# A second chain of adding transfers in the room of spent input combinations, a product ahead of two attention tiles, and a fixed order for the joining

## The chip, the cores and the metric

The kernel runs on one core of one Trainium2 chip, in one launch. The metric is the device time in microseconds, as the median of several runs. A profile is one such execution taken by the hardware profiler; its span, from the first to the last record, is a little shorter than its time.

## The reference

One decoder layer for a sequence of 256 tokens of width 1024 (all float32):

```python
mod = silu(c) @ w_ada + b_ada                # shift, scale, gate: 1024 each
h = rmsnorm(x, norm_g) * (1 + scale) + shift
q, k, v, g_attn, cb, cc, cx, g_conv, m_attn, m_conv = split(h @ w_in)   # ten blocks of 1024 columns
attn = softmax(q k^T / sqrt(128) + bias, causal) v         # 8 heads of 128, one block of 256 keys
y_attn = (attn * silu(g_attn)) @ w_o_attn
y_conv = (cb * conv3(cc * cx) * silu(g_conv)) @ w_o_conv
merged = sigmoid(m_attn) * y_attn + sigmoid(m_conv) * y_conv
return rmsnorm(x + gate * (merged @ w_out), final_g)
```

## The kernel before

**Precision.** Each product of float32 matrices is three products in fp32r: a matrix is split into a high part (ScalarE, "ACT", copies it to fp32r: the `h` tiles of line 74) and a low part (VectorE, "DVE", subtracts: the `l` tiles of line 75), and TensorE ("PE") takes high times high, high times low, low times high. So every MB of weights costs one ACT copy and one DVE subtraction of 128x2048 elements ahead of its matmuls. The `h` and `l` tiles stand in rings of three buffers each: the split of one unit can begin when the matmuls of the unit three before it are done. The raw weights come through a ring of five buffers of 1 MB (`RAW_BUFS`), loaded from SP's queue; a buffer is free when its split is done.

**The work in order.** Adaptive norm; q and k; v; then twelve units of 256 columns for `cc`, `cx`, `cb` with the attention heads between them; four units `gc`, four `ga`; from here on the stage that the change touches. It holds `m_conv` (named `mc`), `m_attn` (tiles `ma00` to `ma11`), `w_o_attn` (tiles `oa00` to `oa11`), `w_o_conv` (`oc`) and `w_out` (`o00` to `o11`). A tile such as `ma01` is 512 of the 1024 rows of the weight against 512 columns, for both halves of the tokens: 24 matmuls. Two tiles make one half of the columns.

**Seven products.** `mc` and `oc` are computed with seven products of 12 matmuls each where eight would be usual (a Strassen-Winograd scheme, class `Seven`, methods `p7 p5 p1 p6 p2 p4 p3`; on PE the products show as `mcp7h`, `ocp3l` and so on). Four of the seven take combinations of the input's quarters (`combos`: two big tiles, `sxhV` and `sxhBI` for `mc`, `sxcV` and `sxcBI` for `oc`; the first of the two holds what p7 and p5 read, the second what p6 and p3 read). Some take sums of weight blocks, and these sums are made by transfers that add: POOL's queue loads one block into the tile `sum` (shown as `mcsum`, `ocsum`, line 544) and adds another to it (line 509); the tile `first` (`mct`, `oct`) is loaded on SP and added to by POOL. `p7` reads `sum`, then POOL adds a third block for `p6`, and DVE adds one more for `p4`. Both chains use the same big tile, named by its tag W2, so `ocsum` waits until `mcp4l` (the low part of `mc`'s p4) has read `mcsum`.

**Joining.** `SA` becomes sigmoid(m_attn) times y_attn, `SC` becomes sigmoid(m_conv) times y_conv (lines 634 and 620). `joined(n)` (line 687) adds them for one half n of the columns, `turned(n)` transposes the sum on PE (`pm`, line 711) and splits it into `M` (lines 353 and 354), and `M` times w_out gives `ao`. `wo_split` loads and splits w_out; for its second half the last 256 columns are multiplied with the gate first (line 700, `gf`). The gate is a column tile `gcol`; to get it as a row, PE transposes it (`pgt`), ACT copies it (`grow`), ACT's queue stores it (`gd`) and loads it back to all partitions (`gf`, line 683), which takes W2 after `ocsum`.

**What sets the order.** The tile framework sorts each engine's instructions by priority and readiness, except those wrapped in `pin`, which keep the order of the program. PSUM banks come from a ring of five (`bank`), apart from banks 0 to 2, which the seven products hold.

Of the kernel before, what the change touches and what calls it, by code (L numbers as in the profile page):

```python
# [11 lines left out]
F32 = mybir.dt.float32  # L12
F32R = mybir.dt.float32r
AF = mybir.ActivationFunctionType
ALU = mybir.AluOpType
PSUM = bass.MemoryType.PSUM

P = 128
D = 1024
S = 256  # L20
NH = 8
KT = D // P
# [13 lines left out]
UNIT = {key: i for i, key in enumerate(UNITS)}  # L36
# [3 lines left out]
def layer_kernel(ctx: ExitStack, tc, x, c, vec, wp_all, slab_all, onehot, final_g, out):  # L40
    nc = tc.nc
    x, out = x[0], out[0]

    const = ctx.enter_context(tc.tile_pool(name="const", bufs=1))
    big = ctx.enter_context(tc.tile_pool(name="big", bufs=1))
    wp = ctx.enter_context(tc.tile_pool(name="wp", bufs=3))
    tp = ctx.enter_context(tc.tile_pool(name="tp", bufs=2))
# [6 lines left out]
    def bank(name, at=None):  # L54
        if at is None:
            at = ring[turn[0] % len(ring)]
            turn[0] += 1
        return ps.tile([P, 512], F32, tag=f"b{at}", name=name)
# [19 lines left out]
    pin = tc.keep_in_program_order  # L78

    H = big.tile([P, KT, 512], F32R, tag="H", name="H")  # L80
    QK = big.tile([P, 2 * NH, S], F32, tag="QK", name="QK")
    V = big.tile([P, 2, D], F32, tag="V", name="V")
# [7 lines left out]
    ident = const.tile([P, P], F32, name="ident")  # L90
# [6 lines left out]
    gcol = const.tile([P, KT], F32, name="gcol")  # L97
# [181 lines left out]
    for i in range(KT):  # L279
# [7 lines left out]
        a, b = span(0), span(1)  # L287
# [64 lines left out]
    def put(src, dst, j, pin=lambda i: i):  # L352
        pin(nc.scalar.activation(dst[:, 2 * j:2 * j + 2, 0:S], src, AF.Copy))  # L353
        pin(nc.vector.tensor_sub(dst[:, 2 * j:2 * j + 2, S:], src, dst[:, 2 * j:2 * j + 2, 0:S].bitcast(F32)))
# [111 lines left out]
    n = 0  # L466
# [25 lines left out]
    def gated(blk, src, dst, j):  # L492
        g = unit((blk, j), H, tmp("cc", f"{blk}{j}"))
        sg = tmp("y", f"s{blk}{j}")
        nc.scalar.activation(sg, g, AF.Silu)
        nc.vector.tensor_mul(sg, sg, src[:, 2 * j:2 * j + 2, :])
        put(sg, dst, j)
# [8 lines left out]
        return [bank(f"a{blk}{n}{t}") for t in range(2)]  # L506

    def add_on(t, key):
        nc.gpsimd.dma_start(t, wp_all[UNIT[key]], accum_op=ALU.add)

    def combos(x, name):
        f = raw_tile([P, 2048], "f" + name).rearrange("p (k n) -> p k n", k=KT)
        nc.vector.tensor_add(f, x[:, :, 0:S].bitcast(F32), x[:, :, S:].bitcast(F32))
        out = {}

        def quarter(t, kh):
            return f[:, 4 * kh:4 * kh + 4, t * P:(t + 1) * P]

        def combo(i, op, a, b, tag):
            v = tp.tile([P, 4, P], F32, tag=tag, name=f"v{name}{i}", bufs=2)  # L520
            op(v, a, b)
            dst = homes[i // 3][:, i % 2]
            nc.scalar.activation(dst[:, :, 0:P], v, AF.Copy)
            nc.vector.tensor_sub(dst[:, :, P:], v, dst[:, :, 0:P].bitcast(F32))
            out[i] = dst
            return v

        homes = [big.tile([P, 2, 4, S], F32R, tag=tag, name=f"sx{name}{tag}") for tag in ("V", "BI")]
        v1 = combo(1, nc.vector.tensor_sub, quarter(1, 0), quarter(1, 1), "cx")
        combo(0, nc.vector.tensor_sub, quarter(0, 0), quarter(1, 0), "cc")  # L530
        v2 = combo(3, nc.vector.tensor_sub, v1, quarter(0, 0), "y")
        combo(4, nc.vector.tensor_add, v2, quarter(0, 1), "cx")
        return {3: out[0], 1: out[1], 2: out[3], 4: out[4]}

    class Seven:
        def __init__(self, blk, x, sink):
            self.blk, self.x, self.sink = blk, x, sink

        def key(self, r, c):
            return (self.blk, c - 1, r - 1)  # L540

        def begin(self):
            self.sum = big.tile([P, 2048], F32, tag="W2", name=self.blk + "sum")
            nc.gpsimd.dma_start(self.sum, wp_all[UNIT[self.key(1, 2)]])  # L544
            add_on(self.sum, self.key(2, 2))

        def begin_first(self):
# [65 lines left out]
    def part(x, t, n):  # L613
        return x[:, t, 512 * n:512 * (n + 1)]
# [9 lines left out]
    def tile(blk, n, kh):  # L624
        if kh == 0:
            banks[blk] = pair(blk, n)
        a = banks[blk]
        rows_tile(blk, n, kh, GA if blk == "oa" else H, a)
        if kh and blk == "ma":
            for t in range(2):  # L630
                nc.scalar.activation(part(SA, t, n), a[t], AF.Sigmoid)
        elif kh:
            for t in range(2):
                nc.vector.tensor_mul(part(SA, t, n), part(SA, t, n), a[t])

    mc, oc = Seven("mc", H, to_gate), Seven("oc", GC, to_merge)
    mc.begin()
    ring[:] = range(3, 8)
    turn[0] = 0
    for j in range(4):  # L640
        gated("gc", YB, GC, j)
        if j < 2:
            run_slot(n + j)
        if j == 1:
            mc.begin_first()
            mc.sx = combos(H, "h")
    SC = big.tile([P, 2, D], F32, tag="YB", name="SC")
    gated("ga", AT, GA, 0)
    mc.p7()
    gated("ga", AT, GA, 1)  # L650
    mc.p5()
    gated("ga", AT, GA, 2)
    mc.p1()
    mc.p6()
# [2 lines left out]
    mc.p2()  # L657
    tile("ma", 0, 0)
    mc.p4()
    oc.begin()  # L660
    tile("ma", 0, 1)
    mc.p3()
    oc.sx = combos(GC, "c")
    tile("ma", 1, 0)
    oc.begin_first()
    oc.p7()
    tile("ma", 1, 1)
    oc.p5()
# [3 lines left out]
    tile("oa", 0, 1)  # L672
    oc.p2()
    oc.p4()
    gf = big.tile([P, 2 * D], F32, tag="W2", name="gf")
    gb, fg = gf[:, 0:D], gf[:, D:]
    pgt = bank("pgt")
    nc.tensor.transpose(pgt[0:KT, 0:P], gcol, ident)
    grow = tp.tile([KT, P], F32, tag="mx", name="grow")
    nc.scalar.activation(grow, pgt[0:KT, 0:P], AF.Copy)  # L680
    gd = tc.dram_tile([KT, P], F32, name="gd")
    nc.scalar.dma_start(gd, grow)
    nc.scalar.dma_start(gb, bass.AP(tensor=gd.tensor, offset=gd.offset, ap=[[0, P], [1, D]]))

    def joined(n, ts=range(2)):
        for t in ts:
            nc.vector.tensor_add(part(SA, t, n), part(SA, t, n), part(SC, t, n))

    joined(0)
    tile("oa", 1, 0)  # L690
    oc.p3()
    M = big.tile([P, KT, 512], F32R, tag="H", name="M")
    wo = {}
# [1 line left out]
    def wo_split(n, kh, pin=lambda i: i):  # L695
        raw = load(("wo", n, kh), f"wo{n}{kh}").rearrange("p (k n) -> p k n", k=4)
        if n:
            g = gb[:, D - S:]
            g = bass.AP(tensor=g.tensor, offset=g.offset, ap=[g.ap[0], [0, 4], g.ap[1]])
            pin(nc.vector.tensor_mul(raw[:, :, S:], raw[:, :, S:], g))  # L700
        wo[n, kh] = split(raw, [P, 4, 512], f"o{n}{kh}", 1, pin)
# [3 lines left out]
    def turned(n):  # L705
        for j in range(2 * n, 2 * n + 2):
            pm = bank(f"pm{j}")
            for k in range(2 * j, 2 * j + 2):
                for t in range(2):
                    c0 = (k % 2) * S + t * P  # L710
                    nc.tensor.transpose(pm[:, c0:c0 + P], MR[:, t, k * P:(k + 1) * P], ident)  # L711
            put(pm.rearrange("p (a b) -> p a b", a=2), M, j)

    turned(0)
    tile("oa", 1, 1)
    joined(1)
    ring[:] = range(8)
    for kh in range(2):
        wo_split(0, kh)
    XR = big.tile([P, 2, D], F32, tag="V", name="XR")  # L720
    nc.sync.dma_start(XR, x.rearrange("(t p) d -> p t d", p=P))

    TT = big.tile([P, 2, D], F32, tag="BI", name="TT")
# [39 lines left out]
    for n in range(2):  # L763
        w2 = [wo[n, kh] for kh in range(2)]
        if n == 0:
            ao = [bank(f"ao{t}") for t in range(2)]
            for kh in range(2):
                for t in range(2):
                    rows_mm(ao[t], M, t, *w2[kh], 4 * kh, slice(0, 512), kh == 0, kh == 1)
                    if kh == t == 0:  # L770
                        turned(1)
                        wo_split(1, 0, pin)
                        wo_split(1, 1)
            for t in range(2):
                pregain(t, residual(ao[t], t, 0, 512, 4 * t))
        else:
            tot = partial(0, 1)
            a = bank("ao2")
            for kh in range(2):
                rows_mm(a, M, 0, *w2[kh], 4 * kh, slice(0, 512), kh == 0, kh == 1)  # L780
            cols = residual(a, 0, 512, 512, 1)
            ms = tp.tile([P, 1], F32, tag="ms", name="ms0")
            nc.vector.scalar_tensor_tensor(ms, s8[:, 1:2], 1.0 / D, tot, op0=ALU.mult, op1=ALU.add)  # L783
            finish(0, ms, cols)
            a = bank("ao3")[:, 0:S]
            for kh in range(2):
                rows_mm(a, M, 1, *w2[kh], 4 * kh, slice(0, S), kh == 0, kh == 1)
            pregain(1, residual(a, 1, 512, S, 5))
            tot = partial(4, 2)
            a = bank("ao4")[:, 0:S]  # L790
            for kh in range(2):
                rows_mm(a, M, 1, *w2[kh], 4 * kh, slice(S, 2 * S), kh == 0, kh == 1)
            ms = tp.tile([P, 1], F32, tag="ms", name="ms1")
            finish(1, ms, residual(a, 1, D - S, S, 6, ms, 1.0 / D, tot))
# [69 lines left out]
```

## Time and profile before

| | |
|---|---|
| median of 3 runs | 323.45 us (323.25 to 324.83) |
| profiled execution: its time, its span | 323.24 us, 321.3 us |
| PE busy | 308.2 us, 96% of the span |
| DVE, ACT, POOL busy | 264.9, 199.6, 13.8 us |
| mean granted TensorE clock | 0.996 of full speed |
| DMA moved | 81.13 MB, 252 GB/s over the span |

A row of the timeline has the start, the duration, the engine, the line, the operation with out<-in and shape, and in brackets the idle time of the engine before it with what ended it. In a row of waits stand the total, the number of times and the longest. PE's records overlap: a matmul is recorded for longer than the step to the next one, so a gap is best taken from start to start. SPq, POOLq and ACTq are an engine's issues of transfers.

### The profile page before, as it was taken

The numbers are of one execution on the slowest core, as the hardware profiler recorded it, in microseconds if no ns is written. First come the engines' busy times: TensorE is split into PE (matmuls) and PEld (weight loads), VectorE is DVE, ScalarE is ACT, GpSimd is POOL, SyncE is SP. The second block draws the span as 40 slices with busy tenths as digits, with TensorE's granted clock in tenths as the row PEclk, the third lists the DMA queues.
The fourth block names the chain that finished last, engine by engine and source line by source line (L and its number), as shares of the span: only waits on it lengthen the run. The fifth ranks groups of instructions, "written<-read, shape, count | busy, mean of one in ns | idle before, by whom it ended". The sixth has DMA issues, their size and how long they took to land.

```text
span 321.3 us, 4588 instructions
## 1 busy us (share of the span) xinstructions
PE 308.2 (96%) x1766; PEld 270.3 (84%) x1766; DVE 264.9 (82%) x367; ACT 199.6 (62%) x292; POOL 13.8 (4%) x25
## 2 busy tenths in 40 slices
PE   7799999999999999999999999999997999998992
PEld 6699999888888989888898888888875888886892
DVE  4799994968599899795977988999938779968784
ACT  2665565863677877576777866678937654451430
POOL 2400000000000000110000000000201000000010
PEclk9999999999999999999999999999999999999998
DMA  7999999986675494999335597327899998530003
GB/s 268 412 409 409 407 416 415 401 354 238 247 261 225 179 326 152 392 190 312 155 131 171 222 218 306 132 114 279 220 277 332 345 397 321 216 116 0 0 2 131
DMA packets 15339, 81.13 MB, mean 252 GB/s; under 512 B 1638, under 2 KB 3030, under 8 KB 8150
## 3 DMA queue, kind: packets, MB, share of 16 engines
q1 hardware_dynamic: 12528, 70.40, 56.3%
q0 software_dynamic: 1184, 8.40, 11.7%
q10 hardware_dynamic: 1606, 2.05, 1.9%
q8 instruction: 14, 0.23, 0.3%
q14 instruction: 7, 0.06, 0.0%
HBM read 79.77 MB, written 1.06 MB: 252 GB/s over the span
## 4 chain that ended last, share of the span: by engine, by line
PE 69%; DVE 12%; DMA 8%; issue 5%; ACT 3%; POOL 1%; SPq 0%; POOLq 0%; ACTq 0%; DVEq 0%
PE acc L202 15%; PE agc L346 5%; PE acc L346 5%; PE acx L346 5%; PE acb L346 5%; DMA ocsum<-in_wp_dram 4%; PE acx L348 2%; PE agc L348 2%; PE acb L348 2%; PE acc L348 2%; PE aga L346 2%; PE av L361 2%; PE av L363 2%; PE av L362 2%; DMA xx<-in_x_dram 2%
## 5 line engine op out<-in xcount | busy, mean ns | idle before, releaser
L387 DVE CUSTOM_DVE_ANT_0 gate<-gate,wide,vT 128x1024 f32<-128x1024 f32 x8 | 10.2, 1279 | 0.0
L165 DVE CUSTOM_DVE_ANT_0 ada<-ada,wide,msc 128x1024 f32<-128x1024 f32 x7 | 9.4, 1342 | 0.0
L165 DVE CUSTOM_DVE_ANT_0 ada<-ada,wide,vT 128x1024 f32<-128x1024 f32 x7 | 8.9, 1278 | 0.0
L353 ACT ACTIVATE M<-pm 128x512 fp32r<-128x512 f32 x4 | 2.2, 591 | 9.0 <-PE pm L711 9.0
L332 ACT ACTIVATE lowcb<-acb 128x256 f32<-128x256 f32 x8 | 3.0, 375 | 6.5 <-PE acb L348 6.5
L75 DVE TENSOR_TENSOR ocp7l<-ocsum,ocp7h 128x2048 fp32r<-128x2048 f32 x1 | 2.3, 2291 | 4.9 <-ACT ocp7h L74 4.9
L738 ACT ACTIVATE SQ<-TT 128x512 f32<-128x512 f32 x3 | 1.9, 633 | 6.3 <-DVE TT L733 6.3
L380 ACT ACTIVATE V<-av 128x512 f32<-128x512 f32 x4 | 2.4, 599 | 5.1 <-PE av L363 5.1
L544 POOL DMA_DIRECT2D mcsum<-in_wp_dram x1 | 0.6, 582 | 112.6 <-DVE cc L333 112.6
L75 DVE TENSOR_TENSOR cb0l<-wcb,cb0h 128x2048 fp32r<-128x2048 f32 x1 | 2.3, 2293 | 3.6 <-ACT cb0h L74 3.6
L74 ACT ACTIVATE ocp7h<-ocsum 128x2048 fp32r<-128x2048 f32 x1 | 1.9, 1917 | 4.9 <-DMA ocsum<-in_wp_dram 4.9
L333 DVE TENSOR_TENSOR cc<-acc,lowcc 128x256 f32<-128x256 f32 x8 | 3.4, 422 | 1.8 <-ACT lowcc L332 1.7
L477 ACT ACTIVATE y<-cc,vT 128x256 f32<-128x256 f32 x8 | 3.9, 502 | 1.4 <-DVE cc L473 1.4
L332 ACT ACTIVATE lowcx<-acx 128x256 f32<-128x256 f32 x8 | 3.0, 376 | 2.9 <-PE acx L348 2.8
L143 PE MATMUL wt<-ones 128*128 128x128 f32 x18 | 3.8, 381 | 1.0 <-DVE ones L131 1.0
L756 POOL TENSOR_TENSOR rf<-ms,mhalf 128x1 f32<-128x1 f32 x2 | 1.7, 834 | 72.1 <-DVE ms L783 68.7
L700 DVE TENSOR_TENSOR wo<-wo,gf 128x1024 f32<-128x1024 f32 x2 | 2.4, 1220 | 2.6 <-DMA gf<-gd 2.6
L202 PE MATMUL acc<-hf,slab 128*128 128x256 f32 x16 | 3.9, 386 | 0.7 <-ACT hf L261 0.7
L312 DVE TENSOR_SCALAR QK<-acc 128x512 f32<-128x512 f32 x2 | 1.4, 689 | 3.8 <-PE acc L202 3.8
L403 DVE TENSOR_TENSOR AX<-QK,AX 128x384 fp32r<-128x384 f32 x8 | 4.4, 551 | 0.0
L169 ACT ACTIVATE H<-xnT,scs 128x256 fp32r<-128x256 f32 x7 | 4.1, 588 | 0.3 <-DVE scs L165 0.3
L74 ACT ACTIVATE o00h<-wo 128x2048 fp32r<-128x2048 f32 x1 | 1.9, 1918 | 3.8 <-PE aoa L363 3.8
(557 smaller groups left out, 1150.9 us busy)
## 6 DMA issues: line engine op xcount, KB each, us to landing
ada<-in_wp_dram SPq DMA_DIRECT2D x16, 512.0 KB, 10.3
slab<-in_slab_dram SPq DMA_DIRECT2D x16, 512.0 KB, 10.3
wv<-in_wp_dram SPq DMA_DIRECT2D x4, 1024.0 KB, 11.4
wcc<-in_wp_dram SPq DMA_DIRECT2D x4, 1024.0 KB, 5.9
wcx<-in_wp_dram SPq DMA_DIRECT2D x4, 1024.0 KB, 6.0
gate<-in_wp_dram SPq DMA_DIRECT2D x4, 1024.0 KB, 6.9
wcb<-in_wp_dram SPq DMA_DIRECT2D x4, 1024.0 KB, 5.5
wgc<-in_wp_dram SPq DMA_DIRECT2D x4, 1024.0 KB, 8.7
```

What stands on the lines that cost most here:

```text
L75: pin(nc.vector.tensor_sub(lo[:, s], raw[:, s], hi[:, s].bitcast(F32)))
L165: pin(nc.vector.tensor_tensor_reduce(src, src, csb, vT[:, i:i + 1] if s else 1.0, bias(i, s), ALU.mult, ALU.add, scs[:, i, s:s + 1]))
L169: pin(nc.scalar.activation(dst, xnT[:, i, :], AF.Identity, scale=scs[:, i, 1:2], bias=scs[:, i, 0:1]))
L202: pin(nc.tensor.matmul(acc[j // 2][:, (j % 2) * S:(j % 2 + 1) * S], w[i][:, j * P:(j + 1) * P], x, start=(i == 0 and j // 2 not in opened) ...
L332: nc.scalar.activation(low, a[:, S:], AF.Copy)
L346: nc.tensor.matmul(a, hi[:, k, cols], rhs[:, k, :], start=(k == 0), stop=False)
L348: nc.tensor.matmul(a[:, S:], lo[:, k, cols], rhs[:, k, 0:S], start=False, stop=(k == KT - 1))
L361: nc.tensor.matmul(a, xh, hi[:, k4, cols], start=(first and k4 == 0), stop=False)
L362: nc.tensor.matmul(a, xh, lo[:, k4, cols], start=False, stop=False)
L363: nc.tensor.matmul(a, xl, hi[:, k4, cols], start=False, stop=(last and k4 == 3))
L387: nc.vector.tensor_tensor_reduce(src, src, csb, 1.0, vT[:, 24 + d:25 + d], ALU.mult, ALU.add, gcol[:, d:d + 1])
L403: nc.vector.tensor_sub(lo, src, hi.bitcast(F32))
```

## The change

The second chain (`oc.begin`) is begun right after `mc.p5` and takes the tile with the tag V, which held `mc`'s first input combinations; the combinations of `oc` take W2 and BI in place of V and BI. `oc.begin_first` goes up to right after `mc.p4`. `oc.p3` goes ahead of the tiles `oa10` and `oa11`, and `oa10` goes behind `turned(0)` in the program. The joining, the attention half's product with `SA`, `M`'s splits, the last gate product and its split, and all transfers of POOL are pinned. The gate's transpose and store are done among the `gc` units (j = 1), and its load as a row is issued by POOL, into V, after `oc.p4`.

```diff
     def add_on(t, key):
-        nc.gpsimd.dma_start(t, wp_all[UNIT[key]], accum_op=ALU.add)
+        pin(nc.gpsimd.dma_start(t, wp_all[UNIT[key]], accum_op=ALU.add))
-    def combos(x, name):
+    def combos(x, name, tags):
...
         def begin(self):
-            self.sum = big.tile([P, 2048], F32, tag="W2", name=self.blk + "sum")
-            nc.gpsimd.dma_start(self.sum, wp_all[UNIT[self.key(1, 2)]])
+            self.sum = big.tile([P, 2048], F32, tag=self.home, name=self.blk + "sum")
+            pin(nc.gpsimd.dma_start(self.sum, wp_all[UNIT[self.key(1, 2)]]))
...
-                nc.vector.tensor_mul(part(SA, t, n), part(SA, t, n), a[t])
+                pin(nc.vector.tensor_mul(part(SA, t, n), part(SA, t, n), a[t]))
-    mc, oc = Seven("mc", H, to_gate), Seven("oc", GC, to_merge)
+    mc, oc = Seven("mc", H, to_gate, "W2"), Seven("oc", GC, to_merge, "V")
...
         if j == 1:
+            pgt = bank("pgt")
+            nc.tensor.transpose(pgt[0:KT, 0:P], gcol, ident)
+            grow = tp.tile([KT, P], F32, tag="mx", name="grow")
+            nc.scalar.activation(grow, pgt[0:KT, 0:P], AF.Copy)
+            gd = tc.dram_tile([KT, P], F32, name="gd")
+            nc.scalar.dma_start(gd, grow)
             mc.begin_first()
-            mc.sx = combos(H, "h")
+            mc.sx = combos(H, "h", ("V", "BI"))
...
     mc.p5()
+    oc.begin()
...
     mc.p4()
-    oc.begin()
+    oc.begin_first()
     tile("ma", 0, 1)
     mc.p3()
-    oc.sx = combos(GC, "c")
+    oc.sx = combos(GC, "c", ("W2", "BI"))
     tile("ma", 1, 0)
-    oc.begin_first()
     oc.p7()
...
-    gf = big.tile([P, 2 * D], F32, tag="W2", name="gf")
+    gf = big.tile([P, 2 * D], F32, tag="V", name="gf")
-    pgt = bank("pgt")
-    nc.tensor.transpose(pgt[0:KT, 0:P], gcol, ident)
-    grow = tp.tile([KT, P], F32, tag="mx", name="grow")
-    nc.scalar.activation(grow, pgt[0:KT, 0:P], AF.Copy)
-    gd = tc.dram_tile([KT, P], F32, name="gd")
-    nc.scalar.dma_start(gd, grow)
-    nc.scalar.dma_start(gb, bass.AP(tensor=gd.tensor, offset=gd.offset, ap=[[0, P], [1, D]]))
+    pin(nc.gpsimd.dma_start(gb, bass.AP(tensor=gd.tensor, offset=gd.offset, ap=[[0, P], [1, D]])))
...
-            nc.vector.tensor_add(part(SA, t, n), part(SA, t, n), part(SC, t, n))
+            pin(nc.vector.tensor_add(part(SA, t, n), part(SA, t, n), part(SC, t, n)))
     joined(0)
-    tile("oa", 1, 0)
     oc.p3()
...
-            put(pm.rearrange("p (a b) -> p a b", a=2), M, j)
+            put(pm.rearrange("p (a b) -> p a b", a=2), M, j, pin)
     turned(0)
+    tile("oa", 1, 0)
     tile("oa", 1, 1)
...
-    XR = big.tile([P, 2, D], F32, tag="V", name="XR")
+    XR = big.tile([P, 2, D], F32, tag="W2", name="XR")
...
-                        wo_split(1, 1)
+                        wo_split(1, 1, pin)
```

**On SP's queue**, the loads from `mc`'s p2 on (`wmc`, `wma`, `oct`). Before:

```order
L65 DMA wmc_2253<-in_wp_dram 128x2048
L65 DMA wma_2274<-in_wp_dram 128x2048
L65 DMA wma_2326<-in_wp_dram 128x2048
L65 DMA wmc_2358<-in_wp_dram 128x2048
L65 DMA wma_2400<-in_wp_dram 128x2048
L65 DMA oct_2430<-in_wp_dram 128x2048
L65 DMA wma_2453<-in_wp_dram 128x2048
```

and after:

```order
L65 DMA wmc_2262<-in_wp_dram 128x2048
L65 DMA wma_2283<-in_wp_dram 128x2048
L65 DMA oct_2332<-in_wp_dram 128x2048
L65 DMA wma_2335<-in_wp_dram 128x2048
L65 DMA wmc_2367<-in_wp_dram 128x2048
L65 DMA wma_2409<-in_wp_dram 128x2048
L65 DMA wma_2459<-in_wp_dram 128x2048
```

`oct` has moved ahead of `ma01`, p3's weights and `ma10`; since the raw ring has five buffers, each of these three now takes a buffer that comes free one split later.

**On DVE**, from the low part of `oa10` to `M`'s first low parts. Before:

```order
L75 TENSOR_TENSOR oa10l<-woa_2658,oa10h 128x2048
L620 TENSOR_TENSOR SC<-SC,ocA 128x512
L75 TENSOR_TENSOR ocp3l<-woc_2688,ocp3h 128x2048
L605 TENSOR_TENSOR ocq_2553<-ocB,ocq_2553 128x512
L687 TENSOR_TENSOR SA<-SA,SC 128x512
L620 TENSOR_TENSOR SC<-SC,ocq_2553 128x512
L75 TENSOR_TENSOR oa11l<-woa_2723,oa11h 128x2048
L687 TENSOR_TENSOR SA<-SA,SC 128x512
L700 TENSOR_TENSOR wo_2810<-wo_2810,gf 128x4x256
L610 TENSOR_TENSOR ocq_2450<-ocC,ocq_2450 128x512
L75 TENSOR_TENSOR o00l<-wo_2757,o00h 128x2048
L620 TENSOR_TENSOR SC<-SC,ocq_2450 128x512
```

and after:

```order
L75 TENSOR_TENSOR ocp3l<-woc_2656,ocp3h 128x2048
L620 TENSOR_TENSOR SC<-SC,ocA 128x512
L75 TENSOR_TENSOR oa10l<-woa_2693,oa10h 128x2048
L605 TENSOR_TENSOR ocq_2559<-ocB,ocq_2559 128x512
L610 TENSOR_TENSOR ocq_2456<-ocC,ocq_2456 128x512
L620 TENSOR_TENSOR SC<-SC,ocq_2559 128x512
L687 TENSOR_TENSOR SA<-SA,SC 128x512 x2
L620 TENSOR_TENSOR SC<-SC,ocq_2456 128x512
L75 TENSOR_TENSOR oa11l<-woa_2723,oa11h 128x2048
L354 TENSOR_TENSOR M<-pm_2677,M 128x2x256
L354 TENSOR_TENSOR M<-pm_2684,M 128x2x256
L75 TENSOR_TENSOR o00l<-wo_2757,o00h 128x2048
```

The two splits have changed places, the two additions of the joining stand in a row behind p3's result (L610), and the product of the gate with `wo` (L700) has left this place. Further on, `o01l` now stands ahead of both products of `SA` with `aoa`, where it stood between them.

**On PE**, around the first eight transposes `pm`. Before, from the end of p3:

```order
L560 MATMUL ocC<-ocp3l,sxcBI 128x512
L560 MATMUL ocC<-ocp3h,sxcBI 128x512
L711 MATMUL pm_2709<-ident,SA 128x128 x4
L711 MATMUL pm_2716<-ident,SA 128x128 x4
L361 MATMUL aoa_2656<-oa11h,GA 128x512
L362 MATMUL aoa_2656<-oa11l,GA 128x512
```

and after, where p3 ends ahead of `oa10`, from the tenth of the 24 matmuls of `oa10`:

```order
L361 MATMUL aoa_2691<-oa10h,GA 128x512
L710 MATMUL pm_2677<-ident,SA 128x128
L710 MATMUL pm_2684<-ident,SA 128x128
L362 MATMUL aoa_2691<-oa10l,GA 128x512
L363 MATMUL aoa_2691<-oa10h,GA 128x512
L710 MATMUL pm_2677<-ident,SA 128x128 x3
L710 MATMUL pm_2684<-ident,SA 128x128 x3
L361 MATMUL aoa_2692<-oa10h,GA 128x512
```

The transposes stood between two products; now they stand inside `oa10`. The second eight stand after 12 matmuls of `ao` in one piece, where they stood after 15 in two pieces.

More of the change, by code (lines that the diff above doesn't have):

```diff
@@ L526, in combo @@
             return v
-        homes = [big.tile([P, 2, 4, S], F32R, tag=tag, name=f"sx{name}{tag}") for tag in ("V", "BI")]
+        homes = [big.tile([P, 2, 4, S], F32R, tag=tag, name=f"sx{name}{tag}") for tag in tags]
         v1 = combo(1, nc.vector.tensor_sub, quarter(1, 0), quarter(1, 1), "cx")
@@ L535, in layer_kernel, with __init__ @@
     class Seven:
-        def __init__(self, blk, x, sink):
-            self.blk, self.x, self.sink = blk, x, sink
+        def __init__(self, blk, x, sink, home):
+            self.blk, self.x, self.sink, self.home = blk, x, sink, home
         def key(self, r, c):
```

## The prediction

> **What bounds the kernel now.** I read the page's head first, then the waits of PE, PE's timeline at the places that they name, and last the chain of waits ahead of each.
>
> ```profile
> span 321.3 us, 4588 instructions
> PE 308.2 (96%) x1766; PEld 270.3 (84%) x1766; DVE 264.9 (82%) x367; ACT 199.6 (62%) x292; POOL 13.8 (4%) x25
> ```
>
> PE is the bound: 13.1 us of the span are not its own. From 60 us on, the waits of PE are three rows:
>
> ```profile
> PE ocB L560 <- DVE ocp7l L75: 1.4, 1, 1.4
> PE ama L362 <- DVE ma11l L75: 1.0, 1, 1.0
> PE pm L711 <- DVE SA L687: 0.9, 1, 0.9
> ```
>
> What else PE idles lies at the start and behind its last matmul. So an edit can gain what these three cost, and little more. PE's timeline there, and from the chain one product of 12 matmuls without a wait:
>
> ```profile
> 240.26 0.39 PE L560 MATMUL ocB<-ocp7h,sxcV 128*128 128x512 f32 x1
> 242.09 0.50 PE L560 MATMUL ocB<-ocp7l,sxcV 128*128 128x512 f32 x1 [1.44 <-DVE ocp7l L75]
> ...
> 244.76 0.39 PE L361 MATMUL ama<-ma11h,H 128*128 128x512 f32 x1
> 246.10 0.50 PE L362 MATMUL ama<-ma11l,H 128*128 128x512 f32 x1 [0.95 <-DVE ma11l L75]
> ...
> 293.85 0.39 PE L363 MATMUL ao<-o00h,M 128*128 128x512 f32 x1
> 295.14 0.44 PE L711 MATMUL pm<-ident,SA 128*128 128x128 f32 x2 [0.90 <-DVE SA L687]
> ```
>
> ```profile
> 251.61 2.72 PE ocC L560 x12
> ```
>
> A step is 2.72/12 = 0.227 us. From start to start, less a step, the gaps cost 1.83-0.23 = 1.60, 1.34-0.23 = 1.11 and 1.29-0.23 = 1.06 us: 3.77 together. The first two have one cause, seen in the chain:
>
> ```profile
> 217.59 2.29 DVE mcp4l L75
> ...
> 220.17 0.57 POOL ocsum L544
> ...
> 225.63 12.09 DMA ocsum<-in_wp_dram
> 237.80 1.93 ACT ocp7h L74
> ```
>
> `ocsum` shares its tile with `mcsum`, so its load waits for mcp4l, the adding takes 12.09 us more, and ACT waits for the sum; what stands behind ocp7h on ACT and DVE, ma11's split among it, is late with it.
>
> **Part 1: the second chain from V.** Its load now waits for the last matmul of mc's p5, and its adding for that load:
>
> ```profile
> 198.94 0.39 PE L560 MATMUL mcC<-mcp5h,sxhV 128*128 128x512 f32 x1
> DMA to landing us min/median/max: 5.2/12.0/12.1
> 232.30 0.60 ACT L631 ACTIVATE SA<-ama 128x512 f32<-128x512 f32 x1 [0.39 <-PE ama L363]
> 239.75 2.29 DVE L75 TENSOR_TENSOR ocp7l<-ocsum,ocp7h 128x2048 fp32r<-128x2048 f32 x1 [4.90 <-ACT ocp7h L74]
> 243.76 2.29 DVE L75 TENSOR_TENSOR ma11l<-wma,ma11h 128x2048 fp32r<-128x2048 f32 x1
> ```
>
> (The second row is of the tile ocsum: its load 5.2, its addings 12.0 and 12.1.) Sum ready at 199.3+5.2+12.1, about 218 with POOL's issues. ACT is free for ocp7h at 232.9, ends it at 234.8; DVE, idle for 4.90 us ahead of ocp7l, has been free since 234.85 and ends it at 237.1. PE comes to the low part at 240.49: cover 3.3 us, the 1.60 go. ma11l ended 6.30 after ocp7l's start, so now at 241.2; PE wants it at 240.26+2.72+0.23 = 243.2: the 1.11 go too. What stands ahead of PE then, up to oa01, follows it: each split starts when the product three before it has ended. The third block, for p6, goes out behind ocp7l, so 2.6 us earlier where PE is 2.71 earlier: its cover stays as it was. XR's load moves to W2, which the same p5 frees that freed V: nothing. Gain 2.71, bounds 0 (something else is late there) and 2.71.
>
> What SP pays: `oct` goes ahead of three loads. The worst off is ma10, which issued at 213.37 and now waits for ma00's split:
>
> ```profile
> 213.37 0.33 SPq L65 DMA_DIRECT2D wma<-in_wp_dram  x1
> 215.39 2.28 DVE L75 TENSOR_TENSOR ma00l<-wma,ma00h 128x2048 fp32r<-128x2048 f32 x1
> 227.05 1.91 ACT L74 ACTIVATE ma10h<-wma 128x2048 fp32r<-128x2048 f32 x1
> 234.82 0.39 PE L361 MATMUL ama<-ma10h,H 128*128 128x512 f32 x1
> DMA to landing us min/median/max: 5.4/6.2/6.2
> oct<-in_wp_dram POOLq DMA_DIRECT2D x1, 1024.0 KB, 18.9
> ```
>
> (The fifth row is of the tiles wma.) Issue at 217.7, landing at 223.9 by the longest of its kind, ahead of ACT's 227.05: cost nothing. That cover is gone at 13 us of landing, since 234.82+0.23 less 1.91 and 2.29 is 230.8. The upper bound is the longest landing in the trace, 18.9 us: 5.8 us of wait on PE.
>
> **Part 2: p3 ahead of oa10.** PE's work is the same. DVE makes p3's low part in the place of oa10's and the other way round:
>
> ```profile
> 272.97 2.28 DVE L75 TENSOR_TENSOR oa10l<-woa,oa10h 128x2048 fp32r<-128x2048 f32 x1
> 275.93 0.27 PE L678 MATMUL pgt<-ident,gcol 128*8 128x128 f32 x1
> 277.97 0.69 DVE L605 TENSOR_TENSOR ocq<-ocB,ocq 128x512 f32<-128x512 f32 x1
> 278.57 0.68 DVE L687 TENSOR_TENSOR SA<-SA,SC 128x512 f32<-128x512 f32 x1
> ```
>
> In the clock of before, p4 ends on PE at 275.93 (the pgt row). p3's low part, in the first row's place, is ready at 275.25, wanted at 276.16. oa10's, in the next split's place, ends at 277.97+0.09 = 278.06, wanted at 275.93+2.72+0.23 = 278.88. Both covered, by 0.8 us or more.
>
> **Part 3: the first joining.** The transposes now stand after ten matmuls of oa10, at 278.65+2.27 = 280.92. DVE does L610 on p3's result (p3's last matmul ends at 278.65+0.16), then L620, then the first SA; at 0.60 a step, as between the last two rows, and 0.69 for the last that is 278.85+1.20+0.69 = 280.74. Cover 0.2 us, the thinnest of all. Bounds: nothing, and one split that slips in ahead, 2.28-0.2 = 2.1 us. I take nothing, since DVE stands there back to back and in this order.
>
> **Part 4: the second joining.** It was late since o01l stood between the two products with aoa:
>
> ```profile
> 291.60 2.29 DVE L75 TENSOR_TENSOR o01l<-wo,o01h 128x2048 fp32r<-128x2048 f32 x1
> 293.80 0.68 DVE L634 TENSOR_TENSOR SA<-SA,aoa 128x512 f32<-128x512 f32 x1
> ```
>
> In the new clock (2.71 less) oa10 begins at 275.94, and oa11, with some 1.0 for transposes, ends at 275.94+10.9+1.0 = 287.9. On DVE the first joining ends at 278.6; L620, oa11l, M twice, o00l, o01l follow (0.6+2.2+1.2+2.2+2.2), to 287.0; then aoa's two products, the second not before 288.1, and two additions: 288.1+0.6+0.6+0.69 = 290.0. PE comes to the transposes at 287.9+12x0.227 = 290.6. Cover 0.6: the 1.06 go; bounds 0 and 1.06.
>
> **Part 5: the gate row and the tail.** pgt, grow and gd move to an earlier stage, where ACT has waits for PE of its own; PE's one extra transpose is the one removed here: nothing, both ways within 0.3 us. The load of gf ended a wait of DVE, not of PE, but it pushed everything behind it:
>
> ```profile
> DVE wo L700 <- DMA gf<-gd: 2.6, 1, 2.6
> 298.16 1.22 DVE L700 TENSOR_TENSOR wo<-wo,gf 128x1024 f32<-128x1024 f32 x1
> ```
>
> From POOL it is issued behind ocp4l, near 267.4, and wanted only by L700, at 293.6 (below): 26 us of cover against 18.9 for the longest landing. Against this speaks the Trainium skill, "SBUF — State Buffer", section "Summary: rules for kernel authors", which advises to issue from ACT or SP a transfer that is to hide under DVE, since descriptors written for POOL's queue can starve while DVE holds a shared port. Here the trace does not bear it out:
>
> ```profile
> 216.00:225.00 9.00, 9.00 (x41) 7.46 (x40) 9.00 (x6) 8.19 (x9) 0.57 (x1) 1.00 0.79 291
> ```
>
> DVE is busy for all 9.00 of these 9 us (the second group is PE's loads, the third DVE), and POOL's load of 220.17 landed in 5.2.
>
> The pins cost something here. Both gate products (L700) now stand in the last stage, o11's after o10's split. From the first transpose to L700 it took 298.16-295.14 = 3.0 us, so L700 can start at 290.6+3.0 = 293.6. Then: product 1.2, o10h 1.9, o10l 2.3, to 299.0 (PE, after ao's 48 steps and the transposes' 0.9, wants it at 287.9+10.9+0.9+0.2 = 299.9); product to 300.2, o11h to 302.1, four TT of 0.6 to 302.6, o11l to 304.9. PE wants that after 13 more steps and 15 of half the width, at 299.7+2.95+1.7 = 304.4. And at the end DVE has one more 0.6 us step between ao's last halves. I charge 0.35 for both; bounds 0 and 1.1 (0.5 and 0.6).
>
> **The sum.** 1.60+1.11+1.06-0.35 = 3.42 against the profiled execution's own 323.24 (its span and 1.9 around it; 0.21 under the median of 323.45): 319.8 us.
>
> **The rivals.**
> - *The thin joining.* The transposes inside oa10 wait, since DVE is later than by my count. For it: 0.2 us of cover, and PE can't pass them. Against it: DVE's row there holds no wait for DMA any more. Price 1.0 (two steps of 0.6 less the cover) to 2.0 (a split): 320.8 to 321.8. Chance 0.16.
> - *The gap moves.* The sum is there, but the next in line holds PE at the same places: ACT or DVE, both behind by their rings. For it: ma11's gap had its own row. Against it: 2.0 us of cover. One or two of the three gaps stay (1.11 to 2.2): 320.9 to 322.0, and with the joining's 1.0 up to 323.0; the point in the middle is 322.2. Chance 0.12. By the rule of the Trainium skill named above, starved addings of POOL would be one way into this case.
> - *Slower: weights behind the second chain.* ma10's load, 4.3 us later, meets the adding of oct on the DMA engines and lands as late as that did, 18.9: ACT and then PE wait 5.8 us at the first matmul of ma10, 319.8+5.8 = 325.6. It decides from 18.3 on (3.4+1.6 of wait). Against it: the wma tiles landed within 6.2, the last of them with ocsum's adding of 225.63 beside it. Chance 0.06.
>
> **Numbers.** What a measurement of this kernel can tell from no change is some 0.5%, 1.6 us. My forecast has 0.66 (319.2 to 320.7; its floor is 323.24-3.77 = 319.5 with a spread of 0.3). Faster: 0.66 and the first rival's 0.16, 0.82; same 0.12; slower 0.06. The range holds forecast and first rival, 0.82: 319.1 to 321.9.
>
> **What would show it.** Right: ocsum's load issues near 199.5 and no wait of ACT for it is left; PE's rows show no gap at ocp7l and ma11l; `M`'s second transposes follow the twelfth matmul of ao without one; PE's busy share goes to 97%. Wrong: a wait of PE for `SA` inside oa10, or for o11l near the end; ma10h on ACT waiting for DMA; a landing of ocsum's third block, or of gf, beyond 18 us.

## The result, and where the time went

The changed kernel takes 318.83 us (median of 4 runs, 318.65 to 319.20) against 323.52 for the kernel before (4 runs, 323.25 to 324.83): a ratio of 0.9849 with a 95% interval of 0.9820 to 0.9877. That is 4.7 us, where I had forecast 3.4, and 0.3 us under the low end of my range. The profiled execution took 318.78, its span 317.0, so 4.3 us less span than before. Timed once more it took 319.27 (6 runs) against 323.16 (11 runs): 3.9 us less, ratio 0.9887 (0.9863 to 0.9911); that 319.27 lies inside my range of 319.1 to 321.9.

The head of the page, and its line on the chain that ended last:

```profile
span 317.0 us, 4590 instructions
PE 307.7 (97%) x1766; PEld 271.0 (85%) x1766; DVE 264.5 (83%) x367; ACT 199.8 (63%) x292; POOL 15.3 (5%) x26
...
PE 94%; DMA 2%; ACT 1%; issue 1%; POOL 1%; SPq 0%; DVE 0%; POOLq 0%
```

PE's busy time hardly moved (307.7 us against 308.2), but from 60 us on its list of waits, which had three rows in the kernel before, is empty. The second chain's transfers on POOL, ACT's and DVE's splits of `ocsum`, and PE there:

```profile
199.22 0.57 POOL L544 DMA_DIRECT2D ocsum<-in_wp_dram  x1 [14.82 <-PE mcC L560]
207.08 0.86 POOL L509 DMA_DIRECT2D ocsum<-in_wp_dram  x1 [7.29 <-DMA ocsum<-in_wp_dram]
...
266.92 0.56 POOL L683 DMA_DIRECT2D gf<-gd  x1 [29.12 <-DVE ocp4l L75]
```

```profile
226.68 1.92 ACT L74 ACTIVATE ma10h<-wma 128x2048 fp32r<-128x2048 f32 x1
...
232.38 1.91 ACT L74 ACTIVATE ocp7h<-ocsum 128x2048 fp32r<-128x2048 f32 x1
```

```profile
234.35 2.29 DVE L75 TENSOR_TENSOR ocp7l<-ocsum,ocp7h 128x2048 fp32r<-128x2048 f32 x1
...
238.36 2.29 DVE L75 TENSOR_TENSOR ma11l<-wma,ma11h 128x2048 fp32r<-128x2048 f32 x1
```

```profile
239.85 0.39 PE L560 MATMUL ocB<-ocp7h,sxcW 128*128 128x512 f32 x1
240.08 0.39 PE L560 MATMUL ocB<-ocp7l,sxcW 128*128 128x512 f32 x1
...
242.80 0.39 PE L362 MATMUL ama<-ma11l,H 128*128 128x512 f32 x1
...
248.01 0.39 PE L560 MATMUL ocC<-ocp5h,sxcW 128*128 128x512 f32 x1
```

The load now waits for mc's p5 and is issued at 199.2. ACT's row of ocp7h, which waited 4.90 us for the adding, and that of ma10h have no bracket. ocp7l ends at 236.64, 3.4 us ahead of its first matmul; ma11l at 240.65, 2.2 ahead. PE's second matmul follows the first by a step.

The second joining and the end of the kernel, on DVE, with PE's transposes and last matmul between:

```profile
286.23 0.68 DVE L634 TENSOR_TENSOR SA<-SA,aoa 128x512 f32<-128x512 f32 x1
287.19 0.69 DVE L634 TENSOR_TENSOR SA<-SA,aoa 128x512 f32<-128x512 f32 x1 [0.28 <-PE aoa L363]
287.79 1.29 DVE L687 TENSOR_TENSOR SA<-SA,SC 128x512 f32<-128x512 f32 x2
```

```profile
289.87 1.03 PE L710 MATMUL pm<-ident,SA 128*128 128x128 f32 x8
...
310.14 0.28 PE L363 MATMUL ao<-o11h,M 128*128 128x256 f32 x1
```

```profile
310.31 0.42 DVE L745 TENSOR_TENSOR TT<-TT,gf 128x256 f32<-128x256 f32 x1
310.64 0.15 DVE L750 TENSOR_TENSOR s<-s 128x1 f32<-128x1 f32 x1
310.71 0.42 DVE L736 TENSOR_TENSOR TT<-ao,XR 128x256 f32<-128x256 f32 x1
```

SA is ready at 289.08, 0.8 us before the transposes. At the end DVE reaches the last residual (L736) 0.57 us after the last matmul's start; before it was 315.18 against 314.86, 0.32.

One table holds nearly all of what follows (in the experiments' kernels line numbers can stand up to 7 higher). PE runs through the same work in every kernel, so its marks cut the span into stages: the start of the first slab matmul (acc); from ocp7h's first matmul to the first of oc's p5 (36 steps); from oa11h's first to o01h's first (48 steps and the second joining's eight transposes); from the last matmul's start to the span's end. Each entry is a difference of starts in that kernel's trace, and the last column is the span without its start; these two take the span as the page gives it, to 0.1, so they are good to 0.05:

```
                   acc    p7 to p5  oa11 to o01  end    span - acc
before            11.92    11.19      13.24      6.44    309.38
before_again      12.12    10.57      13.95      6.51    309.58
chain_alone       11.80     8.16      13.91      6.52    307.10
late_alone        11.93    10.66      11.92      6.87    308.07
gate_alone        11.89    10.42      11.88      6.80    307.51
o11_pinned_alone  11.91    11.68      11.89      6.92    308.99
changed           11.41     8.16      11.94      6.86    305.59
after_again       11.85     8.16      11.93      6.82    305.55
p3_back           11.13     8.16      11.88      7.08    305.67
pins_off          11.11     8.16      11.78      6.90    305.49
gate_late         11.39     8.16      11.81      6.80    305.41
tail_act          11.82     8.16      11.91      6.65    305.38
best              12.14     8.16      11.80      6.56    305.16
dose1_held        12.19     8.91      11.94      6.87    306.41
dose2_held        11.22    15.91      11.93      7.08    313.58
```

Changed against before: 3.03 at the chain, 1.30 at the second joining, less 0.42 at the end, 0.10 for the moved transpose (228.44 from acc to ocp7h against 228.34) and 0.07 around o11l, plus 0.05 elsewhere: 3.79. The other 0.51 of the 4.3 lies ahead of acc. Of the end, 0.31 is DVE's: its last scaling (L758) starts 2.48 us behind the last matmul, where it started 2.17 behind. What follows that scaling took 4.3 to 4.6 us in the kernels of the table, 4.6 in p3_back too, which has no edit there; so differences of 0.3 in the column "end" need not be an edit's.

### The profile page after: what moved, and what is told of

Same layout as the page of the kernel before. It is cut to its first block, busy times and chain, and to the rows that moved or that the text cites. A ratio compares the mean times of both kernels' runs of the same rounds, so it can differ in the third digit from the quotient of the medians.

```text
span 317.0 us, 4590 instructions
## 1 busy us (share of the span) xinstructions
PE 307.7 (97%) x1766; PEld 271.0 (85%) x1766; DVE 264.5 (83%) x367; ACT 199.8 (63%) x292; POOL 15.3 (5%) x26
## 3 DMA queue, kind: packets, MB, share of 16 engines
HBM read 79.77 MB, written 1.06 MB: 255 GB/s over the span
## 4 chain that ended last, share of the span: by engine, by line
PE 94%; DMA 2%; ACT 1%; issue 1%; POOL 1%; SPq 0%; DVE 0%; POOLq 0%
PE acc L202 15%; PE agc L346 5%; PE acc L346 5%; PE acx L346 5%; PE acb L346 5%; PE aga L346 5%; PE mcB L560 3%; PE ocB L560 3%; PE aga L348 2%; PE agc L348 2%; PE acx L348 2%; PE acb L348 2%; PE acc L348 2%; PE av L361 2%; PE aoa L362 2%; PE av L362 2%
## 5 line engine op out<-in xcount | busy, mean ns | idle before, releaser
L544 POOL DMA_DIRECT2D mcsum<-in_wp_dram x1 | 0.6, 578 | 112.6 <-DVE cc L333 112.6
L75 DVE TENSOR_TENSOR ocp1l<-woc,ocp1h 128x2048 fp32r<-128x2048 f32 x1 | 2.3, 2294 | 3.1 <-ACT ocp1h L74 3.1
L509 POOL DMA_DIRECT2D mcsum<-in_wp_dram x2 | 1.8, 888 | 54.4 <-ACT lowgc L332 43.5
L354 DVE TENSOR_TENSOR M<-pm,M 128x512 fp32r<-128x512 f32 x4 | 2.6, 686 | 2.1 <-ACT M L353 2.1
L143 PEld LDWEIGHTS wt<-ones 128*128 128x128 f32 x18 | 3.4, 283 | 1.0 <-DVE ones L131 1.0
L74 ACT ACTIVATE o11h<-wo 128x2048 fp32r<-128x2048 f32 x1 | 1.9, 1922 | 3.6 <-PE ao L363 3.6
L75 DVE TENSOR_TENSOR gc1l<-wgc,gc1h 128x2048 fp32r<-128x2048 f32 x1 | 2.3, 2291 | 2.3 <-ACT gc1h L74 2.3
## 6 DMA issues: line engine op xcount, KB each, us to landing
wv<-in_wp_dram SPq DMA_DIRECT2D x4, 1024.0 KB, 11.3
```

What stands on the lines that cost most here:

```text
L75: pin(nc.vector.tensor_sub(lo[:, s], raw[:, s], hi[:, s].bitcast(F32)))
L143: pin(nc.tensor.matmul(wt[:, 0:P], ones, ones, start=True, stop=True))
```

## The experiments

**The kernels again.** Both as they are, for what moves without any edit.

> The kernel before, unchanged, for the spread of its start: in its first profile x's first piece lets DVE begin at 5.18 us and PE's first slab matmul (acc) starts at 11.92; in the changed kernel 4.80 and 11.41. Theory A (the 0.5 us at the start is chance in the landing of the first loads): acc between 11.3 and 12.0, not the same as in the first profile to 0.1. Theory B (the start is the change's): 11.9 again. Everything between acc and the last matmul within 0.2 of the first profile.

> The changed kernel again, for the same. Theory A: acc's start anywhere from 11.3 to 12.0, and the span moves with it by as much. Theory B: 11.4 again. From acc to the last matmul 298.7 as in the first profile, to 0.2.

acc began at 12.12 and 11.85, so the start moves by itself: over all profiles from 11.11 to 12.46. What moves it is the landing of x's second piece, for acc starts 3.75 us behind ACT's first use of it in the two first profiles as in the others:

```profile
8.17 1.06 ACT L242 ACTIVATE xx<-xx 128x1024 f32<-128x1024 f32 x1 [3.66 <-DMA xx<-in_x_dram]
```

```profile
7.66 1.06 ACT L242 ACTIVATE xx<-xx 128x1024 f32<-128x1024 f32 x1 [3.15 <-DMA xx<-in_x_dram]
```

Theory A (chance in the landing of the first loads) stands for the start, though 12.12 lies just above the 11.3 to 12.0 that I gave it. But "everything between within 0.2" failed for the kernel before; its waits, from 60 us on, were four:

```profile
PE ama L362 <- DVE ma11l L75: 1.0, 1, 1.0
PE pm L711 <- DVE SA L687: 0.9, 1, 0.9
PE ocB L560 <- DVE ocp7l L75: 0.8, 1, 0.8
PE ao L361 <- DVE M L354: 0.5, 1, 0.5
```

The gap at ocp7l was 0.6 smaller, and there was a new wait, for M. The gap at ocp7l hangs on a landing: in the five profiles with the late chain ACT's ocp7h began anywhere from 237.12 to 238.28, when the adding had landed. M's wait is taken up below. The changed kernel's stages repeat to 0.04.

**The chain alone, and all but the chain.** chain_alone is the kernel before with

```diff
-    mc, oc = Seven("mc", H, to_gate), Seven("oc", GC, to_merge)
+    mc, oc = Seven("mc", H, to_gate, "W2"), Seven("oc", GC, to_merge, "V")
...
     mc.p5()
+    oc.begin()
...
-    oc.begin()
+    oc.begin_first()
```

and late_alone is the changed kernel with just these lines put back. In both the tiles that hang on them (the combinations of `oc`, `gf`, `XR`) change places with them; POOL's transfers are pinned in both.

> The kernel before with the second chain in V alone (load, adding and input combinations placed as in the changed kernel; p3, joining, gate row as before). Theory A (my two gaps, under-sized: a wait of PE also slows the steps right behind it): from ocp7h's first matmul to that of ocC's p5 PE takes 36 steps of 0.227, 8.2 us, in place of 11.19, so 3.0 us less; the wait for SA at the second joining stays at 0.9 (about 1.3 with its steps); the time falls by 3.0, to some 320.5. Theory B (the gaps as I sized them, the rest of the gain is in other parts of the change): 2.7 less, 320.8. Rival C (the gap moves): a new wait of PE between 248 and 290, gain under 2.5.

> The changed kernel with the second chain back in W2 (load and adding as late as before); p3 ahead, pins, turned order and gate row as in the changed kernel. Theory A: PE's waits for ocp7l (1.4) and ma11l (1.0) stay, that for SA is gone, worth 1.3 with its slow steps; the stretch behind the last matmul is 0.4 longer than before and o11l costs 0.1: net 0.8 faster, some 322.7. Theory B (the rest of the gain lies in the gate row and its load): 1.5 or more faster, 322.0 or less. Rival C (the late part gives nothing without the chain): within 0.3 of before.

chain_alone: 320.30 against 322.57, ratio 0.9930 (0.9908 to 0.9953). Its stretch from p7 to p5 is 8.16, so 3.03 less than in the first profile of before, as theory A had it (2.41 less than in before_again, whose gap was smaller); the joining took 13.91, with the same two waits as before_again. late_alone: 321.90, ratio 0.9986 (0.9958 to 1.0014), which tells nothing by itself; by stages the joining gave 1.3 (2.0 against before_again) and the end took 0.4 back. Rival C (a gap that moves) is out: no wait came up behind the chain.

**Which part cures the second joining?** Four kernels. p3_back puts `tile("oa", 1, 0)` ahead of `oc.p3()` again in the changed kernel; pins_off takes its three late pins away; gate_late puts its gate row back (transposed behind p4, stored and loaded by ACT); gate_alone is the kernel before with the gate row alone moved (and POOL's transfers pinned).

> The changed kernel with p3 put back behind oa10 (its first transposes follow p3); the pins stay. Theory A (what mattered at the second joining was only that o01l's split came between the two products with aoa; with the pins it stands ahead of both): PE has no wait for SA at the second joining, and the span is within 0.3 of the changed kernel's 317.0. Rival (p3's place is what gave the third gap's 1.3 us): the wait for SA is back with 0.9 or more, span 318.2 or above.

> The changed kernel with the three late pins taken away (the products with aoa, the joining, M's split); p3 stays ahead. The first joining's two additions then stand apart, with L620 and L610 between them, and the first two transposes come three matmuls earlier. Theory A: at the second joining no wait, as in the changed kernel; at the first joining PE comes 0.7 us earlier, 0.4 to 0.5 past the cover of 0.2 that I counted, so a wait for SA of 0 to 0.6: span 317.0 to 317.6. Rival (the pins are what gave the third gap): a wait for SA at the second joining of 0.9 or more, span 318.2 or above.

> The changed kernel with the gate row as before (transposed behind p4, stored and loaded by ACT); everything else as changed. gf then lands some 285 to 286, and DVE needs it first behind M's second split, near 292.3. Theory A (either the early gate row or the new order of DVE's steps is enough): no wait of PE at the second joining or for M, span less its start (acc's first matmul) 305.6 to 305.8. Rival (the early gate row gave the 1.3): the wait for SA is back, 306.5 or more.

> The kernel before with the gate row alone moved (transposed and stored during the gc stage, loaded by POOL); chain in W2, p3, joining and tail's code as before. Theory A (new, from the repeat of the kernel before: DVE's wait for gf is what set the second joining; from L700's start to the transposes it was 9.88 us in each of three runs, and M's wait of 0.5 had the same source): PE has no wait for SA and none for M, and from oa11h's first matmul to o01h's PE takes 12.0 us or less where the two runs of before took 13.24 and 13.95. Theory B (mine of the prediction: o01l between aoa's products was the cause): the wait for SA would go only because o01l now stands ahead of both; then the wait for M may stay. Rival (the gate row is without effect): both waits as before.

None of the four has a wait at the second joining: 11.88, 11.78, 11.81 and 11.88. The repairs are redundant; each of the three can be left out, and the gate row alone suffices. (pins_off had no wait at the first joining either.) That it suffices goes against my reason, the place of o01l. In the kernel before DVE stood as follows (as the trace of before_again has it):

```profile
285.53 1.23 DVE L700 TENSOR_TENSOR wo<-wo,gf 128x1024 f32<-128x1024 f32 x1 [3.28 <-DMA gf<-gd]
...
294.67 1.29 DVE L687 TENSOR_TENSOR SA<-SA,SC 128x512 f32<-128x512 f32 x2
```

No row between them has a bracket: from gf's landing DVE is back to back, and PE's transposes begin 9.88 us after L700 in before (285.26, 295.14), in before_again (285.53, 295.41) and in chain_alone (282.78, 292.66). So gf sets the joining. But in gate_alone o01l had moved ahead too. o11_pinned_alone keeps gf late and only holds o11's gate product behind o10's split:

```diff
-                        wo_split(1, 1)
+                        wo_split(1, 1, pin)
```

> The kernel before with o11's gate product held to its place in the program, behind o10's split; everything else as before, gf's load as late as before, and o01l's split still between the two products with aoa. Theory A (gf's wait of 2.6 to 3.3 in DVE's row set the second joining): DVE does not stand still there, SA is ready 2.6 us sooner, no wait of PE for SA or M; from oa11h's first matmul to o01h's 11.9. Theory B (o01l's place is the cause): the wait for SA stays at 0.5 or more, 12.6 or above. Either way the tail: some 0.4 longer behind the last matmul, as in the changed kernel.

o01l is still between the two products, and PE does not wait, neither for SA nor for M:

```profile
284.49 2.29 DVE L75 TENSOR_TENSOR o00l<-wo,o00h 128x2048 fp32r<-128x2048 f32 x1 [1.35 <-ACT o00h L74]
...
289.16 0.68 DVE L634 TENSOR_TENSOR SA<-SA,aoa 128x512 f32<-128x512 f32 x1
289.76 2.29 DVE L75 TENSOR_TENSOR o01l<-wo,o01h 128x2048 fp32r<-128x2048 f32 x1
291.96 0.68 DVE L634 TENSOR_TENSOR SA<-SA,aoa 128x512 f32<-128x512 f32 x1
```

```profile
PE ocB L560 <- DVE ocp7l L75: 1.8, 1, 1.8
PE ama L362 <- DVE ma11l L75: 1.0, 1, 1.0
```

Theory A is shown: the wait for gf, 2.6 to 3.3 us in DVE's row, was the cause. The edit takes the gate product's own 1.2 us out of that place too, but DVE waits 1.35 us for o00h there now, so the product alone would have fitted in. The same run's end, 6.92 against 6.44 and 6.51, shows what this pin does to it: the last scaling starts 2.60 us behind the last matmul. gate_alone, without the pin, starts it at 2.17 as before; its end of 6.80 comes from what follows the scaling.

**What a wait costs.** dose2 and dose3 write ocp7's low part again on DVE, two and three times; dose2_pinned also holds the steps around it.

> The changed kernel with ocp7's low part written three times on DVE, the same values each time: 2 x 2.2 = 4.4 us later, where the changed kernel has 3.4 us of cover at ocp7l and 2.2 at ma11l. Theory A (a wait of PE costs its gap and 0.15 to 0.2 of slower steps behind it): waits of about 1.0 for ocp7l and 1.2 for ma11l, and from ocp7h's first matmul to ocC's p5 2.4 to 2.7 us more than 8.16, which is 0.3 more than the two gaps start to start less a step; the span longer by the same. Theory B (no cost but the gap): the stretch longer by the two gaps exactly. Rival C (some of it is made good later): span longer by under 2.0.

> The same with ocp7's low part written four times: 6.6 us later. Theory A: waits of 3.2 for ocp7l and 1.2 for ma11l, the stretch 4.6 to 4.9 longer, again some 0.3 above the two gaps: the cost of a restart does not grow with the wait. Theory B: the gaps exactly. A third way: the slower steps grow with the wait, to 0.5 or more.

> The changed kernel with ocp7's low part written three times on DVE, and the order of PE's, ACT's and DVE's steps of ocp7, ma11 and ocp5 held as in the changed kernel, so that only the two waits are put in: cover 3.4 against 4.4. Theory A (a wait costs its gap and 0.15 us of slower steps behind it): gaps of 1.0 at ocp7l and 1.1 at ma11l (start to start less a step 0.227), and from ocp7h's first matmul to ocC's the 8.16 grow by the two gaps and 0.3. Theory B: by the two gaps alone.

All three missed, since the added steps moved others: in dose2 and dose3 PE took p5's first matmul ahead of ma11l and waited 1.4 for ocp5h, in dose2_pinned ACT made ma11h only behind its copy of p7's result. Spans less acc rose by 4.3, 8.0 and 18.9, more than the waits listed for them (1.7, 5.5, 10.6). I do not split all of the rest; a part of dose2's is seen. Seven rows of PE like the first of these were 0.43 apart, though its waits were no longer than those of dose3, where steps stayed at 0.23 there; the second fence is the clock (the last numbers but two):

```profile
244.35 0.63 PE L361 MATMUL ama<-ma11h,H 128*128 128x512 f32 x1
244.77 0.63 PE L362 MATMUL ama<-ma11l,H 128*128 128x512 f32 x1
```

```profile
243.90:246.50 2.60, 2.60 (x8) 1.99 (x7) 2.60 (x2) 0.00 (x0) 0.47 (x1) 0.50 0.79 239
```

dose1_held and dose2_held hold PE's order alone, and no other stage moved but the end (by 0.2, in dose2_held):

```diff
...
+            if nm == "ocp7":
+                for _ in range(1):    # 2 in dose2_held
+                    nc.vector.tensor_sub(lo, rr, hi.bitcast(F32))
```

> The changed kernel with ocp7's low part written twice on DVE, the second time behind the two steps that follow it, and PE's order held; every other step stands where it stood. The low part then ends 0.6 us behind PE's need (240.6 against 240.08 in the first profile's clock); ma11's is in time. Theory A: one gap of 0.5 to 0.7 start to start less a step, and the stretch from ocp7h's first matmul to ocC's 8.16 + gap + 0.15. Theory B: 8.16 + gap.

> The same with the low part written three times, the third behind ma11's low part: it ends at 245.0, so one gap of about 4.9 at ocp7l and none at ma11l. Theory A: 8.16 + gap + 0.15 as after a short wait. Third way (as in dose2_pinned, where 8 steps behind a wait of 2.8 took 0.427 each and the granted clock was 0.52): 8 steps at half the clock, so 8.16 + gap + 1.6 to 1.9, 14.7 to 15.0. Theory B: 13.1.

```profile
240.63 0.39 PE L567 MATMUL ocB<-ocp7h,sxcW 128*128 128x512 f32 x1
241.48 0.50 PE L567 MATMUL ocB<-ocp7l,sxcW 128*128 128x512 f32 x1 [0.45 <-DVE ocp7l L559]
241.81 0.62 PE L567 MATMUL ocB<-ocp7h,sxcW 128*128 128x512 f32 x2
```

```profile
239.66 0.39 PE L567 MATMUL ocB<-ocp7h,sxcW 128*128 128x512 f32 x1
244.91 0.80 PE L567 MATMUL ocB<-ocp7l,sxcW 128*128 128x512 f32 x1 [4.86 <-DVE ocp7l L559]
245.50 1.05 PE L567 MATMUL ocB<-ocp7h,sxcW 128*128 128x512 f32 x2
...
250.56 0.40 PE L363 MATMUL ama<-ma11h,H 128*128 128x512 f32 x1
```

The short wait: start to start less a step 0.85 - 0.23 = 0.62, the stretch 8.91 - 8.16 = 0.75 longer, so 0.13 more than the gap, in the first steps behind it (0.33, then 0.24). The long wait: 5.25 - 0.23 = 5.02, the stretch 7.75 longer, so 2.7 more: 13 steps from 244.91 to 250.56 took 5.65 and not 2.95. Theory A (a wait costs its gap and some 0.15) holds for the short wait and falls for the long one; I had the third way (slower steps at half the clock) at 1.6 to 1.9, which was still too small.

**The end of the kernel.** tail_act leaves the first row tile's last scaling to ACT:

```diff
-        nc.vector.tensor_scalar_mul(TT[:, t, 0:VCUT], TT[:, t, 0:VCUT], r)
+        cut = VCUT if t else 0
+        if cut:
+            nc.vector.tensor_scalar_mul(TT[:, t, 0:cut], TT[:, t, 0:cut], r)
```

with the stores cut alike; best is this and gate_late together.

> The changed kernel with the first row tile's final scaling and store left wholly to ACT (no VCUT part on DVE and SP there), to take a 0.47 us step from DVE ahead of the last residual. Theory A (the stretch behind the last matmul is longer by 0.4 since DVE is late, at L736 0.57 us behind that matmul's start where it was 0.32): L736 starts 0.32 behind, the stretch falls from 6.86 to some 6.5. Rival (ACT's longer store of the first tile, issued near 311, then ends the span): 6.9 or longer.

> The changed kernel with the gate row as before (as in gate_late) and the first row tile's end left to ACT (as in tail_act). If both add: span less acc's start 305.2 (305.57 of the changed kernel's two runs, less 0.16 and 0.19); if not, 305.4 or more.

```profile
310.16 0.42 DVE L745 TENSOR_TENSOR TT<-TT,gf 128x256 f32<-128x256 f32 x1
310.50 0.15 DVE L750 TENSOR_TENSOR s<-s 128x1 f32<-128x1 f32 x1
310.69 0.15 DVE L751 TENSOR_SCALAR s<-s 128x1 f32<-128x1 f32 x1
310.86 0.42 DVE L736 TENSOR_TENSOR TT<-ao,XR 128x256 f32<-128x256 f32 x1
```

In tail_act L736 starts 0.31 behind the last matmul (310.55), as said, and the stretch falls by 0.2 to 6.65, not to 6.5: DVE's last scaling comes 0.31 earlier, but what follows it took 0.1 longer (4.48 against 4.39). Both edits add: 305.16 against 305.57. Timed:

> The kernel best once more, timed beside the changed kernel: 0.4 us below it if the profiles' difference holds (318.3 to 318.6 where the changed kernel has 318.7 to 319.0), and faster than before by 1.4 to 1.6 per cent. Rival: the same within the spread of the start, no difference that can be told.

> The changed kernel, timed as often on the same chip: 1.2 to 1.5 per cent faster than before, by 3.8 to 4.7 us (3.8 to 4.0 is what the profiles show without the start).

best 318.74 (318.25 to 318.96, 6 runs), ratio 0.9872 (0.9846 to 0.9898); changed 319.27 (318.69 to 319.33, 6 runs). That is 0.5 us less; the slowest run of best lies below five of the six of the changed kernel. The stages say the same: 305.16 and 305.14 in the two profiles of best against 305.55 to 305.59 in the three of the changed kernel.

## Why the prediction was right and wrong

*What bounds it, and where it gains: right.* The three waits went and nothing took their place.

*Part 1, the chain: right mechanism, too small.* Cover 3.4 at ocp7l (3.3 said) and 2.2 at ma11l (2.0). The gain was 3.03, not 2.71. The step that failed here is "from start to start, less a step": it leaves out the slower steps behind a wait, 0.17 and 0.14 here, 0.13 in dose1_held. The whole stretch, 11.19 less 36 steps of 0.227, would have given 3.0 from rows that I had. The loads that oct went ahead of cost nothing: ma10h did not wait, so the slower rival is out. The gap that moves is out too: POOL's transfers of `ocsum`, under a busy DVE, landed within 11.7 us, where the longest took 12.1 before. That does not speak against the page that I had named beside it: the Trainium skill, "SBUF — State Buffer", section "Summary: rules for kernel authors", has such starving while DVE is in its 2x or 4x modes, and no row here tells the mode.

```profile
DMA to landing us min/median/max: 7.6/8.6/11.7
```

The third block, for p6, goes out 4.9 us earlier by the rows that I had (242.04 less 237.14), not 2.6; its cover grew, and the sum did not hang on it.

*Parts 2 and 3: right.* No wait at p3, oa10 or the first joining, the thin rival's place. PE began the first transposes at 277.48, which is 280.92 in the clock of before (3.44 back), the number I had.

*Part 4: right in sign, wrong in cause, too small.* 1.30 for 1.06, and the cause was gf, not o01l. I had written that the load of gf ended a wait of DVE, not of PE, and left it there; followed on through DVE's row it is PE's third gap. In two more profiles with the old joining (before_again and chain_alone) PE also waited 0.5 for M, which the first profile did not show, and the stretch was 0.67 to 0.71 longer.

*Part 5: the gate row for nothing was wrong, the end right.* Alone the gate row is worth all of the joining (13.24 or 13.95 to 11.88), but in this change another part would have given it as well, so the sum was spared. The end cost 0.42 and o11l 0.07, for the 0.35 that I charged.

*The sum and its floor: the step that put the time outside the range.* With the terms as measured 3.79, 319.45 us: still in the range. What went below it was the start, 0.51 earlier by the landing of x, for which the sum had no term and the floor of 319.5 only a spread of 0.3; the last 0.1 is what a profiled execution takes around its span, 1.8 and not 1.9. All profiles spread at the start by 1.35; with acc at its earliest, 11.11, the floor would have stood near 318.7. The gaps of before, made by landings, spread as widely: p7 to p5 took 10.42 to 11.68 in the five profiles with the late chain. That the median fell below the range and not into it was, as far as the record shows, chance of this kind: timed once more the same kernel came out inside it, at 319.27. The starts of the executions without a profile are not on record; the 0.51 is that of the two profiled ones. Two figures of the rivals were off and bear on nothing: the middle of 320.9 and 323.0 is 322.0, not 322.2, and 3.4+1.6 of wait are reached at a landing of 18.2, not 18.3.

## What to carry to other kernels

Price a wait by the whole stretch that holds it, against the same count of steps elsewhere, and not by the gap between two starts; and where a gap is made by a transfer's landing, treat its size in one profile as one draw. When an engine that is not the bound stands still, follow its row from there until it meets the bound: if no row between has a wait, that stall is the cause, whatever row the bound names. Where one gap has several cures, each alone may show the whole gain, and together they show it once.

## What the runs showed of the hardware

A wait of PE cost more than its length here, and a long one half as much again (7.75 us for a gap of 5.02). Behind waits of 0.45 to 1.44 us in before and dose1_held the first step took 0.33 to 0.34, the next few 0.23 to 0.24, and the clock stayed at 1.00. Behind 4.86 us it took 13 steps until they were back at 0.23, most of them at 0.43:

```profile
245.00:248.40 3.40, 3.40 (x8) 2.72 (x9) 2.06 (x1) 0.00 (x0) 0.86 (x1) 0.50 0.95 277
```

The Trainium skill, "TensorE: Matmul & The Clock Gate", section "What's actually happening", has such a halving after an idle window of about 3.4 us that runs freely, so that its phase matters. The granted clock of 0.50 agrees, and that the same waits halved it in dose2 and not in dose3 fits such a phase; but no wait needed to last 3.4 us here: dose2's two were 1.4 and 0.3 us, with PE busy for 1.68 of the 3.40 us from 240.5 on, and one of 2.78 us in dose2_pinned halved the clock too (0.50 from 243.3 to 246.4).

The same 1 MB adding transfer, issued at 225.6 to 227.4, was waited for by ACT until 237.1 to 238.3: 9.7 to 12.6 us from issue in the five profiles with the late chain.
